# Attention in three staggered parts, with a second pair of key tiles summed on GpSimd

## The chip, the cores and the metric

The program runs on one core of one Trainium2 chip. The metric is the device time of one execution in microseconds (us). Before the change it is 2156.86 us, the median of three runs (2151.46 to 2158.35).

## The reference

One inference step of a two-layer trunk of width 1024 over 2048 latent tokens and 128 context tokens. Layer 0 mixes by latent attention (4 heads, compressed keys) and by pooling, layer 1 by a gated position mixing. What matters here is the attention of layer 0. For the latent queries it is

```
s = q_nope . k_nope + q_pe . k_pe            (keys: 2048 latent + 128 cached)
p = softmax(s * (128 + 64) ** -0.5)
o_a = p @ v                                  (per head), then o_a * silu(gate_a)
```

all in float32. Context tokens attend to context alone. In the kernel the keys and the values are the 128 wide normalised latents, and the value projection of a head (`Wuv`) comes behind the value product.

## The kernel before

The work runs in stages: projections of layer 0 (until about 523 us), attention (until about 1175 us), then output and input projections of both layers, which keep TensorE full.

Attention works on blocks of 512 queries of one head, 16 in all, and one more block for the context. A block has nine steps: steps 0 to 7 hold two tiles of 128 keys, step 8 the tile of cached keys. The context block has one step. One loop (lines 1251 to 1263) emits, for each index i, `step_scores` of step i and then `step_pv` of step i - 15 (`LAG`).

`step_scores` (line 827): five matmuls for each key tile (lines 818 to 822) into one of two PSUM pairs (psA); ScalarE copies the scores to an SBUF tile `s` (833); VectorE keeps a running maximum per key row (840, 842). After the last step VectorE joins the halves (846), GpSimd takes the maximum over the partitions (`partition_all_reduce`, 850), and ScalarE copies that to PSUM (858).

`step_pv` (line 863): VectorE subtracts the maximum (866) and ScalarE takes the exponential (870). In seven of the nine steps (`SPLIT_PV`: all but 4 and 8) the probabilities are split in two exact parts: ScalarE casts the high part (874) and GpSimd subtracts it for the low part (876, recorded as line 160 on POOL, as every subtraction of the helper `sub`). TensorE multiplies by the values in three passes (177 to 179), or in float32 (902) in steps 4 and 8, and adds up in one PSUM bank, psB. The denominator's sum over key tiles runs on VectorE in PSUM (891, 894, tile psE), except for step 1 (`POOL_SUM`), whose pair GpSimd adds (885).

`finish` (line 906), after the last step: VectorE adds the two sums (908), the sum is split (297, 160), TensorE sums over the partitions with a matrix of ones (914, 915), VectorE inverts (303 to 311), GpSimd multiplies the gate by the inverse (922), ScalarE copies the value product out of PSUM (926), TensorE applies `Wuv` (929), VectorE multiplies by the gate (939), and SP's queue stores the result (941). The gate is loaded through ScalarE's queue, the queries of the next block through GpSimd's (808, 809).

Tiles come from pools with a fixed number of buffers: 17 for `s` and the running maxima (tag h), 7 for the split probabilities and for weights (tag w), 6 for small things (tag e), 4 for queries (tag r), one PSUM bank each for B, C, D and E. Semaphores and the order on each engine come from a scheduler that plans ahead of the run with a model of each instruction's time. It prefers what stands earlier in the source, but emits what it expects to be ready; so the order on an engine can differ from that of the source, and it is fixed once the kernel is built. The first output projection is emitted in the loop's last steps, from index 145 + 9.

Of the kernel before, what the change touches and what calls it, by code (L numbers as in the profile page):

```python
# [14 lines left out]
P = 128  # L15
# [12 lines left out]
LAG = 15  # L28
# [57 lines left out]
POOL_SUM = (1,)  # L86
# [3 lines left out]
# columns of the packed per-feature vectors  # L90
# [11 lines left out]
def segments(o, n):  # L102
    """Pieces (start, length, condition) of a token block: latent tokens first, then context."""
    out = []
    if o < DEC:
        out.append((0, min(n, DEC - o), 0))
    if o + n > DEC:
        s = max(0, DEC - o)
        out.append((s, n - s, 1))
    return out  # L110
# [3 lines left out]
def trunk_kernel(ctx, tc, xT, cols_in, cond_in, ident_in, edge_in, rope_in, w_ada, w_ada_T, w_in_t, w_inp_T, w_pool,  # L114
# [54 lines left out]
    def behind(ins, last):  # L169
        """issue ins behind last, both on one engine"""  # L170
        if last is not None:
            tc.add_manual_dep(ins.ins, last.ins.name, NO_SYNC, reason="issue order")
        return ins

    def mm3(ps, w, x, first, last):
        """ps += w.T @ x with both operands split in two exact parts."""
        PE.matmul(ps, w[0], x[0], start=first, stop=False)  # L177
        PE.matmul(ps, w[0], x[1], start=False, stop=False)  # L178
        PE.matmul(ps, w[1], x[0], start=False, stop=last)  # L179

    # ---------------------------------------------------------------- constants
# [20 lines left out]
    # ---------------------------------------------------------------- scratch  # L202
# [8 lines left out]
    # ---------------------------------------------------------------- modulation  # L211
# [9 lines left out]
    def ada_derive(l, p, c):  # L221
        """what the modulation is used for: amul and gpost, of the conditions c"""
# [8 lines left out]
    def first_ada(parts):  # L231
        """shift and scale of layer 0: one piece of a weight tile at a time"""
# [30 lines left out]
    def late_ada(rows):  # L263
        """the rest of the modulation, feature by feature: rows [c] is SiLU(cond) on all partitions, in pieces"""
# [28 lines left out]
    # ---------------------------------------------------------------- statistics  # L293
    def split1(x, n, alloc, lo_eng=None):
        """[P, n] -> one tile with the high part in slot 0 and the low part in slot 1."""
# [5 lines left out]
    def invert(src, r, n, scale=None):  # L301
        """rows of src are all the same: 1/x, or 1/sqrt(x * scale + eps), once per column, into slot 1 of r."""
# [11 lines left out]
    def total(x, n, pool):  # L314
        """sum over the partitions of x [P, n], on all of them: on Pool, or prepared for TensorE."""
# [6 lines left out]
    def rstd(r, n, d, pool, tag):  # L322
        """1/sqrt(total / d + eps)"""
# [7 lines left out]
    def sumsq_tiles(tiles, n, pool):  # L331
        """sum over the 8 k-tiles (4 pair tiles) of squares."""
# [12 lines left out]
    def modulate(l, bi, tiles, r, out):  # L345
        """tiles (4 pairs, fp32, overwritten) -> split h."""
# [49 lines left out]
    def first_stats():  # L396
        """block 0: x / rms(x), before the modulation is known"""
# [24 lines left out]
    # ---------------------------------------------------------------- streamed weights  # L422
# [20 lines left out]
    def advance(k):  # L443
        """run the next k pieces of the work that trails the matrix products"""
# [10 lines left out]
    def linear_steps(hh, n, pairs, consume, hook=None):  # L455
        """pairs: number of output feature pairs; consume(pair, psum [P,2,n])"""
# [13 lines left out]
    # ---------------------------------------------------------------- layer 0, projections  # L470
    kvscope = ExitStack()
    kvp = kvscope.enter_context(tc.tile_pool(name="kvp", bufs=1))
    # keys: those of the tokens from KCUT on come late, and SiLU(cond) has their places until then
# [22 lines left out]
    def rope(raw, n, ns, tab):  # L496
        """raw [P, n]: rotate the first ns columns; result in a new tile."""
# [118 lines left out]
    def pooling(t0, t1, lo_t, hi_t, alloc=pool_tiles, size=PT):  # L616
        """o_b for tokens [t0, t1) of the sequence [lo_t, hi_t), in steps."""
# [48 lines left out]
    def merges(uq, uk, up):  # L666
# [38 lines left out]
        # cached context keys  # L705
# [80 lines left out]
    # ---------------------------------------------------------------- attention  # L786
# [17 lines left out]
    def attn_load(j):  # L804
        """queries of block j (4 blocks x 4 heads of latent tokens)."""
# [57 lines left out]
    def step_pv(b, p):  # L863
        nt = len(b.tiles[p])
        s = b.s[p]
        i = V.tensor_tensor(out=s[:, :nt], in0=s[:, :nt], in1=b.m[:, None, :].broadcast_to([P, nt, QB]),  # L866
                            op=ALU.subtract)
        if b.h is None and CTX_BEHIND:
            behind(i, g.last_fin)
        S.activation(out=s[:, :nt], in_=s[:, :nt], func=AF.Exp, scale=SM_SCALE)  # L870
        split = p in SPLIT_PV and nt == 2
        if split:
# [3 lines left out]
            sub(V if p in LO_V else G, pl[:, :nt], s[:, :nt], ph[:, :nt])  # L876
        if p == 0:
            b.o = ps1("B")
            b.pool = b.acc = None
        if nt == 1 and p == 0:  # L880
            b.acc = s[:, 0]
# [7 lines left out]
        elif b.acc is None:  # L889
            b.acc = et()[:, 0] if DEN32 else ps1("E")  # L890
            V.tensor_tensor(out=b.acc, in0=s[:, 0], in1=s[:, 1], op=ALU.add)
        else:
            for a in range(nt):
                V.tensor_tensor(out=b.acc, in0=b.acc, in1=s[:, a], op=ALU.add)  # L894
        last_p = len(b.tiles) - 1
        for a, kt in enumerate(b.tiles[p]):
            first, last = p == 0 and a == 0, p == last_p and a == nt - 1
            if split:
                i = SPLIT_PV.index(p)
                mm3(b.o, (Vh[:, i, a], Vl[:, i, a]), (ph[:, a], pl[:, a]), first, last)  # L900
            else:
                PE.matmul(b.o, Vf[:, kt] if kt < 16 else VX[:, kt - 16], s[:, a], start=first, stop=last)
        if p == last_p:
            finish(b)

    def finish(b):
        if b.pool is not None:
            g.last_fin = V.tensor_tensor(out=b.acc, in0=b.acc, in1=b.pool[:, 0], op=ALU.add)
        den = ps1("D")
        if DEN32:  # L910
            PE.matmul(den, f(ones[1]), b.acc, start=True, stop=True)
        else:
            hl = split1(b.acc, QB, et)
            PE.matmul(den, ones[1], hl[:, 0], start=True, stop=False)
            PE.matmul(den, ones[1], hl[:, 1], start=False, stop=True)
        gt = et()
        if b.h is not None:
            store(LD_GT, gt[:, 0], ga_d[b.h, :, b.t0:b.t0 + QB])
        else:
            dma(gt[:, 0].rearrange("p (h n) -> p h n", h=H), ga_d[:, :, DEC:T].rearrange("h p n -> p h n"))  # L920
        rd = invert(den[:, :QB], et(), QB)
        G.tensor_tensor(out=gt[:, 1], in0=gt[:, 0], in1=rd, op=ALU.mult)
        out = ps1("D")
        if O32:
            oh = et()
            S.copy(oh[:, 0], b.o)
            for h in ([b.h] if b.h is not None else range(H)):
                c = slice(0, QB) if b.h is not None else slice(h * P, (h + 1) * P)
                PE.matmul(out[:, c], Wuv[:, h], oh[:, 0, c], start=True, stop=True)
        elif b.h is not None:  # L930
            oh = split1(b.o, QB, et)
            mm3(out, (Wuv[:, 0, b.h], Wuv[:, 1, b.h]), (oh[:, 0], oh[:, 1]), True, True)
        else:
            oh = split1(b.o, QB, et)
            for h in range(H):
                c = slice(h * P, (h + 1) * P)
                mm3(out[:, c], (Wuv[:, 0, h], Wuv[:, 1, h]), (oh[:, 0, c], oh[:, 1, c]), True, True)
        mx = et()
        (G if MX_G else V).tensor_tensor(out=mx[:, 0], in0=out, in1=gt[:, 1], op=ALU.mult)
# [6 lines left out]
    for j in range(16):  # L946
# [3 lines left out]
        b.s = []  # L950
        b.j = j
# [4 lines left out]
    b.s = []  # L956
    b.j = 16
# [12 lines left out]
    # ---------------------------------------------------------------- layer 0 output, layer 1  # L970
# [417 lines left out]
```

## Time and profile before

| what | value |
|---|---|
| median of three runs | 2156.86 us (2151.46 to 2158.35) |
| span of the profiled execution | 2150.6 us |
| the profiled execution's own time | not stated; the timed runs lie 0.9 to 7.8 us above its span |
| TensorE matmul busy | 93% |
| VectorE busy | 74% |
| ScalarE busy | 52% |
| GpSimd busy | 27% |
| attention | 523 to 1175 us |

The span runs from the first instruction's start to the last one's end. The engines are named PE (TensorE), PEld (its weight loads), DVE (VectorE), ACT (ScalarE), POOL (GpSimd) and SP. Busy time is the sum of the instructions' durations. The ends of matmuls are modelled, and spans on POOL, of custom instructions above all, are rough. What is printed as the releaser of an idle time is inferred from semaphore events.

### The profile page before, as it was taken

How to read it: one execution, taken by the hardware profiler on the slowest of the kernel's cores; microseconds unless marked ns; L12 is line 12 of the kernel's file. 1: busy time of each engine (PE TensorE's matmuls, PEld its weight loads, DVE VectorE, ACT ScalarE, POOL GpSimd, SP SyncE). 2: the span in 40 equal slices, each digit the busy share in tenths (PEclk: the TensorE clock that was granted, in tenths of full speed). 3: DMA queues.
4: the chain of work that ended last, by engine and by line, in shares of the span. 5: the costliest groups of instructions: out<-in, count | busy, mean ns of one | idle time of the engine just before them, and what ended most of it. 6: DMA issues, size and time to landing. Idle time of an engine off the chain costs nothing. (4 is left out here: it accounts for less than half of the span.)

```text
span 2150.6 us, 25720 instructions
## 1 busy us (share of the span) xinstructions
PE 1997.9 (93%) x9442; PEld 1647.0 (77%) x9442; DVE 1589.9 (74%) x2191; ACT 1124.1 (52%) x1311; POOL 583.0 (27%) x387
## 2 busy tenths in 40 slices
PE   5998999989889899898978999999999999999997
PEld 2787777888667666676756878888878988889987
DVE  8677989765799989898987677545574657477575
ACT  6644344444566666666665444443354435445555
POOL 2102121322366575656655210011000100010010
PEclk9999999999999999999989999999999999999999
DMA  7675768766111101111114543245433533364363
GB/s 289 220 262 195 268 211 281 245 216 181 38 30 45 30 30 40 30 44 30 41 58 134 184 160 132 81 146 171 141 110 127 196 118 117 118 228 155 128 215 128
DMA packets 123119, 299.55 MB, mean 139 GB/s; under 512 B 12080, under 2 KB 39024, under 8 KB 122992
## 3 DMA queue, kind: packets, MB, share of 16 engines
q1 hardware_dynamic: 96272, 244.16, 33.6%
q0 software_dynamic: 12992, 30.15, 4.7%
q10 hardware_dynamic: 13728, 23.60, 3.5%
q8 instruction: 74, 1.21, 0.2%
q14 instruction: 53, 0.43, 0.1%
HBM read 242.18 MB, written 55.67 MB: 138 GB/s over the span
## 5 line engine op out<-in xcount | busy, mean ns | idle before, releaser
L177 PE MATMUL psA<-h,w 128*128 128x512 f32 (+2 forms) x1600 | 577.6, 361 | 14.0 <-ACT e L598 13.6
L179 PE MATMUL psA<-h,w 128*128 128x512 f32 (+2 forms) x1600 | 574.1, 359 | 4.2 <-DVE w L160 4.2
L160 DVE TENSOR_TENSOR w<-r,w 128x1024 fp32r<-128x1024 f32 x280 | 351.2, 1258 | 286.8 <-PE psA L178 193.9
L178 PE MATMUL psA<-h,w 128*128 128x512 f32 (+2 forms) x1536 | 549.0, 358 | 0.0
L431 ACT CAST w<-r 128x1024 fp32r<-128x1024 f32 x280 | 292.1, 1049 | 274.8 <-PE psA L179 192.7
L177 PEld LDWEIGHTS psA<-h,w 128*128 128x128 f32 x1600 | 303.4, 190 | 54.9 <-ACT e L598 15.4
L179 PEld LDWEIGHTS psA<-h,w 128*128 128x128 f32 x1600 | 303.4, 190 | 43.5 <-DVE w L160 5.7
L178 PEld LDWEIGHTS psA<-h,w 128*128 128x128 f32 x1536 | 291.6, 190 | 35.3 <-issue 0.5
L160 POOL TENSOR_TENSOR w<-h,w 128x1024 fp32r<-128x1024 f32 x112 | 274.6, 2467 | 116.7 <-ACT h L870 84.4
L833 ACT COPY h<-psA 128x1024 f32<-128x1024 f32 (+1 forms) x145 | 139.3, 961 | 152.0 <-PE psA L822 122.7
L870 ACT ACTIVATE h<-h 128x1024 f32<-128x1024 f32 (+1 forms) x145 | 144.7, 1008 | 57.8 <-DVE h L866 57.8
L842 DVE TENSOR_TENSOR h<-psA,h 128x1024 f32<-128x1024 f32 (+1 forms) x112 | 127.5, 1139 | 41.8 <-ACT h L833 41.7
L866 DVE TENSOR_TENSOR h<-h,psC 128x1024 f32<-128x1024 f32 x135 | 154.9, 1147 | 0.7 <-ACT psC L858 0.7
L319 POOL PARTITION_ALL_REDUCE e<-e x19 | 60.1, 3163 | 337.3 <-DVE e L977 81.2
L894 DVE TENSOR_TENSOR psE<-psE,h 128x512 f32<-128x512 f32 x208 | 143.1, 688 | 5.1 <-ACT h L870 2.0
L178 PE MATMUL psB<-w,Vh 128*128 128x512 f32 x224 | 93.2, 416 | 53.1 <-POOL w L160 53.1
L178 PE MATMUL psA<-o,w 128*128 128x512 f32 (+2 forms) x368 | 134.1, 366 | 0.0
L874 ACT CAST w<-h 128x1024 fp32r<-128x1024 f32 x112 | 117.1, 1046 | 4.8 <-PE psB L179 4.2
L179 PE MATMUL psA<-o,w 128*128 128x512 f32 (+2 forms) x304 | 109.1, 361 | 0.0
L177 PE MATMUL psA<-o,w 128*128 128x512 f32 (+2 forms) x304 | 108.9, 361 | 0.0
L177 PE MATMUL psA<-w,h 128*128 128x512 f32 x272 | 106.2, 391 | 0.5 <-ACT o L1142 0.5
L178 PE MATMUL psA<-w,h 128*128 128x512 f32 x272 | 106.1, 390 | 0.0
(290 smaller groups left out, 3641.1 us busy)
## 6 DMA issues: line engine op xcount, KB each, us to landing
r<-in_w_inc_t_dram SPq DMA_DIRECT2D x80, 512.0 KB, 3.5
r<-in_w_in_t_dram SPq DMA_DIRECT2D x60, 512.0 KB, 4.5
r<-in_w_oap_t_dram SPq DMA_DIRECT2D x40, 512.0 KB, 3.5
r<-in_w_incv_t_dram SPq DMA_DIRECT2D x40, 512.0 KB, 4.2
r<-in_w_outc_t_dram SPq DMA_DIRECT2D x40, 512.0 KB, 3.5
r<-in_w_ada_T_dram SPq DMA_DIRECT2D x32, 512.0 KB, 4.6
r<-wp_d SPq DMA_DIRECT2D x20, 512.0 KB, 6.1
h<-in_w_ada_dram SPq DMA_DIRECT2D x16, 512.0 KB, 10.2
```

The source lines that it names most:

```text
L160: eng.tensor_tensor(out=out, in0=a, in1=f(hi), op=ALU.subtract)
L177: PE.matmul(ps, w[0], x[0], start=first, stop=False)
L178: PE.matmul(ps, w[0], x[1], start=False, stop=False)
L179: PE.matmul(ps, w[1], x[0], start=False, stop=last)
L319: G.partition_all_reduce(r[:, 0, :n], x, P, bass_isa.ReduceOp.add)
L431: S.copy(hi, raw)
L833: S.copy(s[:, :nt], ps[:, :nt])
L842: V.tensor_tensor(out=b.run[:, :nt], in0=ps[:, :nt], in1=b.run[:, :nt], op=ALU.max)
L866: i = V.tensor_tensor(out=s[:, :nt], in0=s[:, :nt], in1=b.m[:, None, :].broadcast_to([P, nt, QB]), op=ALU.subtract)
L870: S.activation(out=s[:, :nt], in_=s[:, :nt], func=AF.Exp, scale=SM_SCALE)
L874: S.copy(ph[:, :nt], s[:, :nt])
L894: V.tensor_tensor(out=b.acc, in0=b.acc, in1=s[:, a], op=ALU.add)
```

## The change

`step_pv` is divided. `step_exp` does the subtraction, the exponential, the split and the denominator's sums, 13 steps behind the scores. In a block's last step it also joins the two sums, now into an SBUF tile, splits the joined sum and starts the gate's load. `step_pv` holds the value product alone, two steps behind `step_exp`. `finish` becomes a generator: the denominator, the copy of the value product and the inversion come with the last value product, and the rest (gate times inverse, `Wuv`, product, store) one index later. Step 4's pair is added on GpSimd as well, as two instructions onto the sum of step 1. Branches of settings that are not in use, and comments, are removed. The core of the diff:

```diff
-LAG = 15
+LAG = 13
+PV_BEHIND = 2
...
-POOL_SUM = (1,)
+POOL_SUM = (1, 4)
...
-    def step_pv(b, p):
+    def step_exp(b, p):
+
         nt = len(b.tiles[p])
         s = b.s[p]
-        i = V.tensor_tensor(out=s[:, :nt], in0=s[:, :nt], in1=b.m[:, None, :].broadcast_to([P, nt, QB]),
-                            op=ALU.subtract)
-        if b.h is None and CTX_BEHIND:
-            behind(i, g.last_fin)
+        V.tensor_tensor(out=s[:, :nt], in0=s[:, :nt], in1=b.m[:, None, :].broadcast_to([P, nt, QB]),
+                        op=ALU.subtract)
         S.activation(out=s[:, :nt], in_=s[:, :nt], func=AF.Exp, scale=SM_SCALE)
-        split = p in SPLIT_PV and nt == 2
-        if split:
+        b.parts[p] = None
+        if p in SPLIT_PV and nt == 2:
             ph = wt(F32R)
             S.copy(ph[:, :nt], s[:, :nt])
             pl = wt(F32R)
-            sub(V if p in LO_V else G, pl[:, :nt], s[:, :nt], ph[:, :nt])
+            sub(G, pl[:, :nt], s[:, :nt], ph[:, :nt])
+            b.parts[p] = ph, pl
         if p == 0:
-            b.o = ps1("B")
             b.pool = b.acc = None
+        last_p = len(b.tiles) - 1
         if nt == 1 and p == 0:
-            b.acc = s[:, 0]
+            b.total = s[:, 0]
         elif p in POOL_SUM:
             if b.pool is None:
                 b.pool = et()
...
                 for a in range(2):
                     G.tensor_tensor(out=b.pool[:, 0], in0=b.pool[:, 0], in1=s[:, a], op=ALU.add)
         elif b.acc is None:
-            b.acc = et()[:, 0] if DEN32 else ps1("E")
+            b.acc = ps1("E")
             V.tensor_tensor(out=b.acc, in0=s[:, 0], in1=s[:, 1], op=ALU.add)
         else:
             for a in range(nt):
                 V.tensor_tensor(out=b.acc, in0=b.acc, in1=s[:, a], op=ALU.add)
+        if p == last_p:
+            if b.acc is not None:
+                t = et()
+                V.tensor_tensor(out=t[:, 0], in0=b.acc, in1=b.pool[:, 0], op=ALU.add)
+                b.total = t[:, 0]
+            b.hl = split1(b.total, QB, et)
+            b.gt = et()
+            if b.h is not None:
+                store(LD_GT, b.gt[:, 0], ga_d[b.h, :, b.t0:b.t0 + QB])
+            else:
+                dma(b.gt[:, 0].rearrange("p (h n) -> p h n", h=H), ga_d[:, :, DEC:T].rearrange("h p n -> p h n"))
+
+    def step_pv(b, p):
+        if p == 0:
+            b.o = ps1("B")
         last_p = len(b.tiles) - 1
         for a, kt in enumerate(b.tiles[p]):
-            first, last = p == 0 and a == 0, p == last_p and a == nt - 1
-            if split:
+            first, last = p == 0 and a == 0, p == last_p and a == len(b.tiles[p]) - 1
+            if b.parts[p]:
                 i = SPLIT_PV.index(p)
+                ph, pl = b.parts[p]
                 mm3(b.o, (Vh[:, i, a], Vl[:, i, a]), (ph[:, a], pl[:, a]), first, last)
             else:
-                PE.matmul(b.o, Vf[:, kt] if kt < 16 else VX[:, kt - 16], s[:, a], start=first, stop=last)
-        if p == last_p:
-            finish(b)
+                PE.matmul(b.o, Vf[:, kt] if kt < 16 else VX[:, kt - 16], b.s[p][:, a], start=first, stop=last)
+        b.parts[p] = None
 
     def finish(b):
-        if b.pool is not None:
-            g.last_fin = V.tensor_tensor(out=b.acc, in0=b.acc, in1=b.pool[:, 0], op=ALU.add)
+
         den = ps1("D")
-        if DEN32:
-            PE.matmul(den, f(ones[1]), b.acc, start=True, stop=True)
-        else:
-            hl = split1(b.acc, QB, et)
-            PE.matmul(den, ones[1], hl[:, 0], start=True, stop=False)
-            PE.matmul(den, ones[1], hl[:, 1], start=False, stop=True)
-        gt = et()
-        if b.h is not None:
-            store(LD_GT, gt[:, 0], ga_d[b.h, :, b.t0:b.t0 + QB])
-        else:
-            dma(gt[:, 0].rearrange("p (h n) -> p h n", h=H), ga_d[:, :, DEC:T].rearrange("h p n -> p h n"))
+        PE.matmul(den, ones[1], b.hl[:, 0], start=True, stop=False)
+        PE.matmul(den, ones[1], b.hl[:, 1], start=False, stop=True)
+        oh = et()
+        S.copy(oh[:, 0], b.o)
         rd = invert(den[:, :QB], et(), QB)
+        gt = b.gt
+        yield
         G.tensor_tensor(out=gt[:, 1], in0=gt[:, 0], in1=rd, op=ALU.mult)
         out = ps1("D")
-        if O32:
-            oh = et()
-            S.copy(oh[:, 0], b.o)
-            for h in ([b.h] if b.h is not None else range(H)):
-                c = slice(0, QB) if b.h is not None else slice(h * P, (h + 1) * P)
-                PE.matmul(out[:, c], Wuv[:, h], oh[:, 0, c], start=True, stop=True)
-        elif b.h is not None:
-            oh = split1(b.o, QB, et)
-            mm3(out, (Wuv[:, 0, b.h], Wuv[:, 1, b.h]), (oh[:, 0], oh[:, 1]), True, True)
-        else:
-            oh = split1(b.o, QB, et)
-            for h in range(H):
-                c = slice(h * P, (h + 1) * P)
-                mm3(out[:, c], (Wuv[:, 0, h], Wuv[:, 1, h]), (oh[:, 0, c], oh[:, 1, c]), True, True)
+        for h in ([b.h] if b.h is not None else range(H)):
+            c = slice(0, QB) if b.h is not None else slice(h * P, (h + 1) * P)
+            PE.matmul(out[:, c], Wuv[:, h], oh[:, 0, c], start=True, stop=True)
         mx = et()
-        (G if MX_G else V).tensor_tensor(out=mx[:, 0], in0=out, in1=gt[:, 1], op=ALU.mult)
+        V.tensor_tensor(out=mx[:, 0], in0=out, in1=gt[:, 1], op=ALU.mult)
         if b.h is not None:
             store(ST_MX, mix_d[b.h, :, b.t0:b.t0 + QB], mx[:, 0])
         else:
...
-    for i in range(len(steps) + LAG):
+    finishing = []
+    for i in range(len(steps) + LAG + PV_BEHIND + 1):
         if i < len(steps):
             b, p = steps[i]
             nb = blks.index(b) + 1
...
             step_scores(b, p)
         if i >= POOL_AT:
             drain(pools, 1)
-        if i >= LAG:
-            step_pv(*steps[i - LAG])
+        if 0 <= i - LAG < len(steps):
+            step_exp(*steps[i - LAG])
+        for it in list(finishing):
+            if next(it, it) is it:
+                finishing.remove(it)
+        j = i - LAG - PV_BEHIND
+        if 0 <= j < len(steps):
+            b, p = steps[j]
+            step_pv(b, p)
+            if p == len(b.tiles) - 1:
+                finishing.append(finish(b))
+                next(finishing[-1])
         if i >= len(steps) + OA_AT:
             drain(first, 1)
```

## Rows read from the trace of the kernel before

**Rows 1.** The page of the kernel before: span, and busy time of each engine

```profile
span 2150.6 us, 25720 instructions
...
PE 1997.9 (93%) x9442; PEld 1647.0 (77%) x9442; DVE 1589.9 (74%) x2191; ACT 1124.1 (52%) x1311; POOL 583.0 (27%) x387
```

**Rows 2.** Stretches of attention: PE, PEld, DVE, ACT, POOL busy (x), PEclk, DMA share, GB/s

```profile
523.00:1175.00 652.00, 575.44 (x2270) 425.37 (x2269) 574.65 (x639) 417.43 (x464) 387.25 (x237) 0.97 0.15 45
1100.00:1175.00 75.00, 58.42 (x214) 40.39 (x213) 62.54 (x72) 43.07 (x50) 45.38 (x22) 0.86 0.35 114
```

**Rows 3.** Table by stretches: one steady block, from reduction to reduction

```profile
703.30:740.82 37.52, 34.12 (x139) 25.49 (x138) 34.29 (x39) 25.20 (x29) 22.91 (x12) 1.00 0.12 35
```

**Rows 4.** Waits of 523 to 1175 us: us in total, times, longest

```profile
POOL w L160 <- ACT h L870: 84.4, 12, 7.2
POOL e L850 <- DVE psE L894: 77.7, 13, 6.2
...
PE psB L178 <- POOL w L160: 53.1, 31, 7.6
```

**Rows 5.** Timeline of GpSimd, 695 to 742 us: start, us, what [idle before <-releaser]

```profile
695.01 2.38 POOL L160 TENSOR_TENSOR w<-h,w 128x1024 fp32r<-128x1024 f32 x1 [0.43 <-ACT w L874]
703.30 1.80 POOL L850 PARTITION_ALL_REDUCE e<-e  x1 [5.91 <-DVE psE L894]
712.25 9.88 POOL L160 TENSOR_TENSOR w<-h,w 128x1024 fp32r<-128x1024 f32 x4 [7.15 <-ACT h L870]
722.44 2.40 POOL L160 TENSOR_TENSOR w<-h,w 128x1024 fp32r<-128x1024 f32 x1 [0.31 <-POOL w L160]
725.25 1.30 POOL L922 TENSOR_TENSOR e<-e,e 128x512 f32<-128x512 f32 x1 [0.41 <-DVE e L311]
726.75 2.41 POOL L160 TENSOR_TENSOR w<-h,w 128x1024 fp32r<-128x1024 f32 x1 [0.20 <-PE psB L178]
729.11 1.31 POOL L885 TENSOR_TENSOR e<-h 128x512 f32<-128x512 f32 x1
730.53 0.90 POOL L808 DMA_DIRECT2D r<-q_d  x1
731.44 0.58 POOL L809 DMA_DIRECT2D r<-q_d  x1
732.46 2.38 POOL L160 TENSOR_TENSOR w<-h,w 128x1024 fp32r<-128x1024 f32 x1 [0.44 <-ACT w L874]
740.82 1.81 POOL L850 PARTITION_ALL_REDUCE e<-e  x1 [5.98 <-DVE psE L894]
749.38 9.88 POOL L160 TENSOR_TENSOR w<-h,w 128x1024 fp32r<-128x1024 f32 x4 [6.75 <-ACT h L870]
```

**Rows 6.** The line of the all-reduce: duration ns min/median/max, first and last start

```profile
L850 POOLq MODIFY_POOL_CONFIG  x32: 1/1/54, 547.2 to 1112.5; - x32
L850 POOL PARTITION_ALL_REDUCE e<-e x16: 1803/1803/1807, 553.7 to 1118.4; - x16
```

**Rows 7.** Groups by shape, 500 to 1150 us: busy us, mean ns | idle before

```profile
L894 DVE TENSOR_TENSOR psE<-psE,h 128x512 f32<-128x512 f32 x206 | 141.7, 688 | 5.1 <-ACT h L870 2.0
...
L885 POOL TENSOR_TENSOR e<-h 128x512 f32<-128x512 f32 x16 | 20.8, 1301 | 0.0
...
L160 DVE TENSOR_TENSOR e<-psE,e 128x512 fp32r<-128x512 f32 x15 | 10.2, 679 | 1.3 <-ACT e L297 1.3
```

**Rows 8.** The line of the last maximum: duration ns min/median/max

```profile
L846 DVE TENSOR_TENSOR e<-h x16: 675/2793/4380, 547.4 to 1110.3; 128x512 f32<-128x512 f32 x16
```

**Rows 9.** Timeline of VectorE: from a block's last maximum to its first use

```profile
695.15 2.79 DVE L846 TENSOR_TENSOR e<-h 128x512 f32<-128x512 f32 x1
...
706.45 1.21 DVE L866 TENSOR_TENSOR h<-h,psC 128x1024 f32<-128x1024 f32 x1
```

**Rows 10.** Timeline of GpSimd at the end of attention

```profile
1128.71 2.35 POOL L160 TENSOR_TENSOR w<-h,w 128x1024 fp32r<-128x1024 f32 x1 [6.70 <-ACT w L874]
...
1152.29 3.37 POOL L160 TENSOR_TENSOR h<-e,h 128x1024 fp32r<-128x1024 f32 x1
```

More of the change, by code (lines that the diff above doesn't have):

```diff
@@ L950, in trunk_kernel @@
         b.s = []
+        b.parts = {}
         b.j = j
@@ L956, in trunk_kernel @@
     b.s = []
+    b.parts = {}
     b.j = 16
```

## The prediction

> **What bounds the kernel now.** I read the page first, to see where the stage of the change lies: the span is 2150.6 us and TensorE is busy for 93% of it, so over the whole program TensorE looks like the limit [rows 1]. Then the table by stretches, for attention alone (523 to 1175 us): there TensorE, with its modelled ends, shows 575 of 652 us, VectorE as much, ScalarE 417 and GpSimd 387 [rows 2]. One steady block of queries (nine steps) takes 37.52 us, with 34.12 on TensorE, 34.29 on VectorE and 22.91 on GpSimd [rows 3]. By these shares GpSimd has nearly 15 us free in each block. The waits contradict that: the longest TensorE waits in the stage are for GpSimd's low parts (53.1 us over 31 waits), while GpSimd itself seems to wait 84.4 and 77.7 us, about as often as there are blocks [rows 4]. An engine that others wait for and that itself waits needs a look at its own timeline [rows 5].
>
> That timeline is the heart of the matter. The low part at 695.01 ends at 697.39; the all-reduce of the maxima is shown at 703.30 for 1.80 us; the next low part starts at 712.25. The 5.91 us before it and the 7.15 us after it are printed as waits, the first for a VectorE sum, which the reduction does not need. The same two gaps stand at the next block: 5.98 and 6.75 us [rows 5]. Two pool-configuration instructions belong to each reduction (32 for 16) [rows 6]; the gaps are equal from block to block within 0.4 us, whatever is going on around them. I take them as GpSimd switching its code to the reduction and back, and so as occupied: 712.25 - 697.39 = 14.86 us per block. The rest of the cycle, from 712.25 to 734.84, is seven low parts, two sums or products of 1.30 us and two DMA issues, with idle bits of 0.31, 0.41, 0.20, 0.11 and 0.44 us, together 1.47 us [rows 5]. So GpSimd works for 36.0 of 37.5 us: **GpSimd sets the pace of attention**, at 96%, and TensorE and VectorE follow.
>
> The label of the trace would have it otherwise, so I weigh it against a rule: the Trainium skill, GPSIMD Engine Reference, section Instruction dispatch, says that the first call to freshly loaded code pays a load of about 6 us (5.95) after the pool-configuration instruction, with no visible instruction. By it the gaps are work and the added sums lengthen each block, as in my sum; by the label they are waits and the sums fit into them, which is the first rival below. The trace's 5.91 and 5.98 us agree with the figure.
>
> **The change, part by part.**
> *One more pair on GpSimd.* For each of 16 blocks, VectorE loses two sums into psE (L894, 0.69 us each) and GpSimd gains two of the kind of L885 and L922, 1.30 us each [rows 5, 7]: +2.6 us of GpSimd per block, 41.6 us in all. Nothing covers it except the 1.47 us of idle bits. The VectorE gain, 16 x 2 x 0.69 = 22 us, lies on an engine that has 3.2 us idle per block already and buys nothing while GpSimd leads.
>
> *The total and its split.* The last addition now writes an SBUF tile and the split reads that tile, where it read psE. The subtraction in the split (L160 on VectorE, e<-psE,e, 0.68 us [rows 7]) so gets two SBUF inputs. The trace has such an instruction: L846 took between 0.68 and 4.38 us, 2.79 in the middle [rows 8]; one that started at 695.15 [rows 9], with a GpSimd low part running until 697.39 [rows 5], ended at 697.94. So VectorE can pay from 0 to 2.1 us per block, inside its 3.2 us. GpSimd pays too when it comes second: its low parts took 2.35 us alone and 3.37 us at the end of the stage, where VectorE made such subtractions [rows 10]. I take +0.4 us per block on GpSimd (the four of 712.25 took 9.88 where 4 x 2.35 is 9.40 [rows 5, 10], a block with other such instructions), bounds 0 and 1.0.
> The Trainium skill, SBUF — State Buffer, section Who interferes with whom, says that a VectorE instruction with two SBUF inputs and a GpSimd instruction that reads SBUF exclude each other for a whole instruction; by it the split costs one engine or the other up to a GpSimd instruction, by the row of the old form it costs nothing. The trace's 2.79 beside 0.68 us agree with the rule.
>
> *Value product two steps later.* The same matmuls. The casts and low parts stay with the exponentials; TensorE gets two steps (2 x 37.5 / 9 = 8.3 us) in the source between a low part and its use. That can remove waits of TensorE for GpSimd, up to the 53 us of [rows 4], but they are the shadow of GpSimd's pace: with less delay TensorE would wait elsewhere. Gain 0. The low and high parts live longer in the seven w buffers; three pairs and one tile fit, and three pairs is what the new distance needs, so the buffers fill. If a low part must wait for a product of three steps before, GpSimd idles: bounds 0 and the present 0.31 us twice per block; I take 0.
>
> *Lag 15 to 13.* Maxima would be ready five steps ahead of use rather than seven. The engines do not follow the source order here: seven steps would be 29 us, but L846 stands at 695.15 and the first subtraction of that maximum at 706.45, 11.3 us later, right behind the reduction [rows 9]. So I cost the lag at nothing in the steady part; the prologue and the drain lose two steps each and the middle gains two, about -2 us.
>
> *Block ending in pieces.* The product with the gate (L922) stands a step later, so its 0.41 us wait for VectorE's transpose [rows 5] goes: -0.4 us per block. The gate load moves two steps forward in ScalarE's queue, where casts and exponentials stand behind it; if its e buffer were not free, they would wait. ScalarE is idle for a third of the stage [rows 2], the old issue showed no wait, and I take 0, with one step (4.2 us) per block as the far upper bound, not in the range. The copy of the value sum (ScalarE, before: after the inversion) frees its PSUM bank sooner; TensorE has room, gain 0. The store of the result stays on SP's queue, one step later, with nobody near behind it.
>
> *Sum.* Per block 2.6 + 0.4 - 0.4 = 2.6 us, in 16 blocks 41.6. At the end, TensorE has about 75 - 58.4 = 16.6 us idle between 1100 and 1175 [rows 2], where products of the following projection can move ahead while GpSimd finishes; I count 5 us for that and 2 for the lag. **41.6 - 7 = +35 us.** The profiled span is 2150.6 us; the timed runs lie 0.9 to 7.8 us above it, the median 6.3. The page states no other time of the profiled execution, so I add the difference to the median: 2156.9 + 35 = **2192 us**. Nothing after attention changes.
>
> **The rivals.**
> *GpSimd's gaps are real waits* (faster). Then there are 14.6 us free per block, the sums hide, and VectorE bounds: 34.3 - 1.4 + about 1.2 for the split, 34.1, plus half its present idle, gives a 35.5 us block, -2.0 x 15 = -30: 2127 us. For it: the printed labels. Against: two gaps of constant length, at each reduction. Chance 0.11.
> *The idle bits and the end absorb it* (no change). If all 1.47 us per block vanish (23.5 us) and all of TensorE's 16.6 us idle at the end is filled, 41.6 - 40 = +1.5: 2158 us. For it: most bits are waits on casts or buffers, which a looser order can remove. Against: they recur as short handovers of 0.1 to 0.4 us. It decides only if both come together. Chance 0.09.
> *The total waits behind a reduction* (slower still). The new sums of step 4 may be queued on GpSimd behind the next block's reduction, 14.9 us; the total, on VectorE four steps later, about 16.6 us, then stands still with the next subtractions behind it, and GpSimd runs dry after its backlog of low parts, about two (4.8 us). It decides once the sums stand behind the reduction by more than those 1.7 us. Price: some 2.5 us per block more, 15 x 2.5 = 37: 2229 us. For it: L885 of step 1 already runs late, at 729.11, after five low parts [rows 5]. Chance 0.15.
> *The new distances change no order on the engines.* Then the added sums and the split remain, and the time is the forecast's; it has no number of its own.
>
> **How the numbers follow.** Forecast 0.65, rivals 0.11, 0.09 and 0.15. The forecast's own range is 2172 (the idle bits gone, -20) to 2210 (a split at 1.0 us, +10, and a slower clock at the end, which already is 0.86 in [rows 2], +8). The range takes in the no-change case almost to its number and the third rival: 2160 to 2233. A measurement tells about 0.3% (6.5 us) from no change; faster by more 0.11, within 0.09, slower by more 0.80.
>
> **What would show it.** On GpSimd's timeline, two more sums per block between reductions and a distance of about 40 us from reduction to reduction; the gaps around each reduction again near 6 and 7 us; VectorE's and TensorE's idle per block longer by about 2 us; L160 on VectorE with e<-e above 0.68 us. I am wrong if the period falls below 37.5 us with the two sums in it, or if the gaps around a reduction shrink.

## The result and the profile after

The changed kernel takes 2191.66 us (median of 4 runs, 2191.25 to 2193.67), the kernel before beside it 2155.62 us. The ratio is 1.0167, with a 95% interval of 1.0150 to 1.0184: slower by 36 us. The profiled execution has a span of 2189.6 us, 39.0 us more than before. A span lies about 2 us under the time of its execution (2189.6 under 2191.39), so by estimate the profiled execution of the kernel before took 2152.5 us, 3 us less than its median; that is the difference between 39.0 and 36.

The page of the changed kernel, its span and the busy time of each engine:

```profile
span 2189.6 us, 25719 instructions
...
PE 2015.3 (92%) x9442; PEld 1662.4 (76%) x9442; DVE 1553.7 (71%) x2159; ACT 1127.8 (52%) x1311; POOL 612.4 (28%) x419
```

VectorE has 32 instructions less and GpSimd 32 more, which is the pair of step 4 in 16 blocks. VectorE is 36 us less busy, GpSimd 29 us more, and the program is longer [rows 1]. The table by stretches, one steady block and the last 75 us of attention (columns as in [rows 2]):

```profile
874.66:913.53 38.87, 33.77 (x138) 25.48 (x138) 31.96 (x37) 25.32 (x29) 24.82 (x14) 1.00 0.12 35
1140.00:1215.00 75.00, 56.72 (x190) 38.05 (x191) 51.21 (x58) 38.00 (x44) 35.57 (x18) 0.86 0.35 113
```

The block is 38.87 us where it was 37.52 [rows 3]. VectorE's busy time fell from 34.29 to 31.96 us in it; what it gained became idle time. GpSimd's timeline in the same block of the changed kernel:

```profile
874.66 1.80 POOL L851 PARTITION_ALL_REDUCE e<-e  x1 [5.99 <-DVE e L899]
883.20 4.75 POOL L161 TENSOR_TENSOR w<-h,w 128x1024 fp32r<-128x1024 f32 x2 [6.74 <-ACT h L834]
887.89 1.30 POOL L886 TENSOR_TENSOR e<-h 128x512 f32<-128x512 f32 x1
889.15 4.76 POOL L161 TENSOR_TENSOR w<-h,w 128x1024 fp32r<-128x1024 f32 x2
893.87 2.65 POOL L889 TENSOR_TENSOR e<-e,h 128x512 f32<-128x512 f32 x2
896.47 2.41 POOL L161 TENSOR_TENSOR w<-h,w 128x1024 fp32r<-128x1024 f32 x1
898.83 1.30 POOL L932 TENSOR_TENSOR e<-e,e 128x512 f32<-128x512 f32 x1
900.08 2.39 POOL L161 TENSOR_TENSOR w<-h,w 128x1024 fp32r<-128x1024 f32 x1
902.40 0.90 POOL L809 DMA_DIRECT2D r<-q_d  x1
903.31 0.59 POOL L810 DMA_DIRECT2D r<-q_d  x1
905.17 2.40 POOL L161 TENSOR_TENSOR w<-h,w 128x1024 fp32r<-128x1024 f32 x1 [1.27 <-ACT w L874]
913.53 1.80 POOL L851 PARTITION_ALL_REDUCE e<-e  x1 [5.96 <-DVE e L899]
```

It answers to [rows 5]. The two new sums (L889) take 2.65 us. The gaps on both sides of the reduction are what they were, 5.99 and 6.74 us, with other instructions now printed as their cause. Between them GpSimd stands still for 1.27 us only; the 0.41 us in front of the product with the gate (L932, before L922) are gone. The reductions of all blocks, from the line of the all-reduce in the changed kernel (duration min/median/max, first and last start):

```profile
L851 POOL PARTITION_ALL_REDUCE e<-e x16: 1801/1802/1804, 554.5 to 1150.1; - x16
```

From the start of the first to the start of the last of 16 reductions there are (1150.1 - 554.5) / 15 = 39.71 us a block; before it was (1118.4 - 553.7) / 15 = 37.65 us [rows 6]. That makes 15 x 2.06 = 30.9 us. The first reduction starts 0.8 us later. From the last reduction's start to the end of the span there were 2150.6 - 1118.4 = 1032.2 us; now there are 1039.5, so 7.3 us more. 30.9 + 0.8 + 7.3 = 39.0 us. I call the two parts the **period** (the mean length of a block) and the **end** below, and take them from each run's own lines in the same way.

Three waits of the changed kernel (all of attention; us in total, times, longest):

```profile
DVE e L938 <- POOL e L932: 62.4, 15, 6.8
PE psB L179 <- POOL w L161: 42.9, 21, 5.9
DVE h L868 <- ACT psC L859: 13.2, 13, 4.0
```

TensorE's wait for low parts fell from 53.1 [rows 4] to 42.9 us, without any gain in time. The first one is new in size (6.9 us before): VectorE reaches the product with the gate earlier than GpSimd does.

### The profile page after: what moved, and what is told of

It is laid out like the page before. It is cut to its first block, busy times and chain, and to the rows that moved or that the text cites. A ratio compares the mean times of both kernels' runs of the same rounds, so it can differ in the third digit from the quotient of the medians.

```text
span 2189.6 us, 25719 instructions
## 1 busy us (share of the span) xinstructions
PE 2015.3 (92%) x9442; PEld 1662.4 (76%) x9442; DVE 1553.7 (71%) x2159; ACT 1127.8 (52%) x1311; POOL 612.4 (28%) x419
## 5 line engine op out<-in xcount | busy, mean ns | idle before, releaser
L161 POOL TENSOR_TENSOR w<-h,w 128x1024 fp32r<-128x1024 f32 x112 | 266.5, 2389 | 124.2 <-ACT h L870 34.8
L868 DVE TENSOR_TENSOR h<-h,psC 128x1024 f32<-128x1024 f32 x135 | 153.2, 1150 | 13.2 <-ACT psC L859 13.2
L179 PE MATMUL psB<-w,Vh 128*128 128x512 f32 x224 | 98.3, 439 | 42.9 <-POOL w L161 42.9
L895 DVE TENSOR_TENSOR psE<-psE,h 128x512 f32<-128x512 f32 x176 | 121.6, 691 | 9.5 <-ACT h L870 7.1
L874 ACT CAST w<-h 128x1024 fp32r<-128x1024 f32 x112 | 117.3, 1047 | 18.1 <-PE psB L180 17.1
L819 PE MATMUL psA<-r,K 128*128 128x512 f32 x192 | 87.8, 457 | 40.0 <-DVE h L843 39.7
L178 PE MATMUL psA<-w,h 128*128 128x512 f32 x272 | 106.2, 391 | 0.4 <-ACT o L1143 0.4
```

The costliest lines, as they stand in the source:

```text
L161: eng.tensor_tensor(out=out, in0=a, in1=f(hi), op=ALU.subtract)
L819: PE.matmul(ps, kh, q[0], start=True, stop=False)
L874: S.copy(ph[:, :nt], s[:, :nt])
```

## The experiments

Each is compared with the kernel before, run beside it on the same chip. Ratios carry 95% intervals.

**1. The pair back on VectorE.**

```diff
-POOL_SUM = (1, 4)
+POOL_SUM = (1,)
```

> The changed kernel with step 4's pair back on VectorE, so lag, stagger, split of the total and the ending in pieces remain. Theory (GpSimd sets the pace and the two added sums are the cost): the block loses 2.6 us of GpSimd, 40 us in all, and the time returns to about the kernel before, 2150 to 2160 us. Rival (the stagger, the lag or the SBUF total cost the time): it stays near 2190 us.

2168.17 us, 1.0069 (1.0049 to 1.0088). The pair is worth about 21 of the 36 us, so it is the larger cost, but the rest of the change costs about 15 us by itself: neither expectation held alone. The line of its reductions shows where:

```profile
L851 POOL PARTITION_ALL_REDUCE e<-e x16: 1802/1802/1803, 555.5 to 1121.2; - x16
```

The period is 37.71 us, as before. With a span of 2167.3 us its end is 1046.1 us, 13.9 longer than before. The lag, the stagger, the total and the pieces together do nothing to the steady part and lengthen what follows the last reduction.

**2. The pair on GpSimd in the kernel before.**

```diff
-POOL_SUM = (1,)
+POOL_SUM = (1, 4)
```

> The kernel before with nothing changed but step 4's pair on GpSimd. Theory: +2.6 us per block less what its 1.47 us of idle bits absorb, 20 to 42 us, so 2176 to 2198 us. Rival (the new distances are the cost, and GpSimd has room): within 6 us of 2156.

2206.63 us, 1.0245 (1.0228 to 1.0261): more than the theory allowed, and slower than the changed kernel. The reductions, and the waits of attention that grew:

```profile
L850 POOL PARTITION_ALL_REDUCE e<-e x16: 1802/1802/1803, 553.2 to 1165.8; - x16
```

```profile
ACT psC L858 <- POOL e L850: 108.0, 15, 9.6
DVE h L866 <- ACT psC L858: 94.8, 13, 9.1
```

The period is 40.84 us, 3.2 more than before, where two sums are 2.6. VectorE now waits 94.8 us for the maxima (0.7 before, 13.2 in the changed kernel). In GpSimd's queue the sums stand in front of the next block's reduction:

```profile
716.70 1.80 POOL L850 PARTITION_ALL_REDUCE e<-e  x1 [6.29 <-PE psA L822]
725.53 9.47 POOL L160 TENSOR_TENSOR w<-h,w 128x1024 fp32r<-128x1024 f32 x4 [7.04 <-ACT h L870]
736.71 1.29 POOL L922 TENSOR_TENSOR e<-e,e 128x512 f32<-128x512 f32 x1 [1.71 <-DVE e L311]
...
741.89 2.67 POOL L888 TENSOR_TENSOR e<-e,h 128x512 f32<-128x512 f32 x2
...
757.87 1.80 POOL L850 PARTITION_ALL_REDUCE e<-e  x1 [6.65 <-PE psA L822]
```

This block is 41.17 us long, 3.65 more than that of [rows 5]. The two sums are 2.67 of it, the gaps around the reduction about 0.6 (7.04 and 6.65 us for 7.15 and 5.98), and GpSimd's idle bits 0.2: 1.71 us in one wait for VectorE's inversion, for 1.47 in five bits. So the sums were added in full and no idle bit took them in. VectorE's wait for the maxima lies on an engine that is busy for 30.37 of the 41.17 us; no run shows that it costs time by itself.

**3. A second, unused reduction in each block.**

```diff
+    g.extra = qpool.tile([P, P], F32, name="extra")
...
-            sub(V if p in LO_V else G, pl[:, :nt], s[:, :nt], ph[:, :nt])
+            lo = G.tensor_tensor(out=pl[:, :nt], in0=s[:, :nt], in1=f(ph[:, :nt]), op=ALU.subtract)
+            if p == 2:
+                behind(G.partition_all_reduce(g.extra, ident, P, bass_isa.ReduceOp.max), lo)
```

> The kernel before with a second, unused all-reduce of a constant 128x128 tile in each of 16 blocks, queued on GpSimd behind the low part of step 2; nothing waits for it but GpSimd's own queue. Theory (the gaps on both sides of a reduction are GpSimd changing its code): 13 to 15 us more per block, +190 to +230 us. Rival (the gaps are waits for data): only the instruction itself, at most 1.8 us per block, so at most +29 us.

2344.88 us, 1.0891 (1.0870 to 1.0911): +191 us, where waits would have given 29 at most. Around one of the added reductions:

```profile
816.17 0.72 POOL L879 PARTITION_ALL_REDUCE extra<-ident  x1 [5.92 <-issue]
823.66 1.28 POOL L888 TENSOR_TENSOR e<-h 128x512 f32<-128x512 f32 x1 [6.77 <-issue]
```

The instruction takes 0.72 us and reads a constant, and still it has 5.92 us before it and 6.77 us behind it: 13.4 us, in which nothing was there to wait for. The gaps are GpSimd's own time. This settles the reading of [rows 5] on which the forecast stands. The 5.92 us agree with the load of about 6 us that the Trainium skill, GPSIMD Engine Reference, section Instruction dispatch, gives for the first call to freshly loaded code. Here such a time falls on each change of code, in both directions.

**4. No reduction.**

```diff
-            ar = G.partition_all_reduce(m[:, 1], src, P, bass_isa.ReduceOp.max)
...
-                b.m = m[:, 1]
+                b.m = src
...
-                S.copy(b.m, m[:, 1])
+                S.copy(b.m, src)
```

> The kernel before without the all-reduce: each partition's own maximum is used, so the maximum over the partitions is left out. Theory: GpSimd has 14.9 us less per block and no longer leads; the next engine, VectorE at about 34 us a block, sets the pace: -2 to -4 us per block, 2095 to 2125 us. Rival (gaps are waits, something else sets the pace): less than 10 us faster.

2115.54 us, 0.9821 (0.9806 to 0.9836), as the theory expected. A stretch of 34.5 us in its steady part shows what leads then, VectorE at 33.96 and TensorE at 33.35 us (columns as in [rows 2]):

```profile
700.00:734.50 34.50, 33.35 (x137) 25.35 (x137) 33.96 (x36) 25.58 (x29) 22.97 (x12) 1.00 0.14 39
```

**5. The block ending in one piece.**

```diff
     def finish(b):
+        yield from ()
...
         gt = b.gt
-        yield
...
-                next(finishing[-1])
+                next(finishing[-1], None)
```

> The changed kernel with the block ending in one piece again, two sums on GpSimd kept. The trace after the change shows VectorE held 62.4 us by the product with the gate on GpSimd (L932), 15 times. If GpSimd's pace is what counts, this wait is a shadow and the time stays within 6 us of 2192; if the pieces cause the drain's extra 10 us, it comes to about 2180 us.

2195.5 us, 1.0184 (1.0150 to 1.0217), not told from the changed kernel's 1.0167. The ending in pieces neither costs nor gains, and the pieces are not what the end lost. VectorE's wait for the gate's product is still there, 59.0 us over 15 times, so this run doesn't show what it would give to be rid of it; that it is a shadow of GpSimd's pace is argued, not shown.

**6. No stagger, the pair moved.**

```diff
-LAG = 13
-PV_BEHIND = 2
+LAG = 15
+PV_BEHIND = 0
```

> The changed kernel with LAG 15 and PV_BEHIND 0: no distance between exponential and value product; the total in SBUF, the pieces and the two sums on GpSimd stay. Theory (in the steady part GpSimd sets the pace, and the old order lets the reduction wait behind the two sums, as in the kernel before with the pair moved, 2206.6 us): about 2200 us, so the stagger is worth 10 us or more where the pair is moved. Rival (the stagger costs the drain 15 us and nothing else): about 2177 us.

2213.37 us, 1.0258 (1.0233 to 1.0284), more than the expected 2200. The stagger and the shorter lag save about 20 us where the pair is moved, nearly all of it in the period (40.91 for 39.71 us). Two waits of this run:

```profile
POOL w L161 <- PE psB L179: 33.9, 13, 5.3
DVE h L868 <- ACT psC L859: 64.0, 13, 7.4
```

The first is on the engine that leads: low parts wait for a value product of TensorE, once in nearly every block. In the changed kernel this is 0.7 us, and waits of low parts for their cast (L874) take its place with 18.0 us. The difference, 15 us, is most of the 18 us that the period gives. The second, VectorE's wait for the maxima (13.2 us in the changed kernel), comes with it; whether it stands behind the first isn't shown.

**7. Lag 13 in the kernel before.**

```diff
-LAG = 15
+LAG = 13
```

> The kernel before with LAG 13 alone. Theory (the engines' order follows readiness, and GpSimd sets the pace): within 8 us of 2154. Rival (the lag is what costs the changed kernel without the moved pair its 15 us): about 2168 us.

2169.86 us, 1.0063 (1.0040 to 1.0086): the rival. The reductions run from 553.6 to 1120.9 us, a period of 37.82 us, and the span is 2163.9, so the end is 1043.0 us, 10.8 more than before; by the medians the run is 12.5 us longer. Here, too, the steady part is what it was. In this kernel the loop is two indices shorter and gives the output projection four pieces instead of six; the changed kernel gives it seven and its end is still longer than before, so that alone is not the cause.

**8. Five split steps in the kernel before.** Steps 3 and 7 go through TensorE in float32.

```diff
-SPLIT_PV = (0, 1, 2, 3, 5, 6, 7)
+SPLIT_PV = (0, 1, 2, 5, 6)
```

> The kernel before with steps 3 and 7 in float32 instead of three passes of split operands: two low parts fewer per block on GpSimd (4.9 us), two casts fewer on ScalarE (2.1 us), 0.7 us more on TensorE. Theory (GpSimd leads at 36 us of 37.5): it falls to 31 us, VectorE leads at about 34.2 us a block, and the time falls by 2.5 to 3.3 us per block, to 2100 to 2115 us, faster than both kernels. Rival (TensorE leads): 0.7 us more per block, about 2165 us.

2119.11 us, 0.9826 (0.9798 to 0.9853): faster than both kernels, 4 us short of the expected gain. One steady block:

```profile
876.75:910.90 34.15, 33.84 (x134) 24.92 (x133) 31.39 (x39) 23.38 (x26) 17.69 (x10) 1.00 0.14 39
```

It takes 34.15 us, and TensorE, with its modelled ends, fills 33.84 of them, VectorE 31.39: with GpSimd relieved, TensorE leads, not VectorE as expected. Over all blocks the period is (1086.5 - 549.6) / 15 = 35.79 us, since the first blocks and the last two are longer.

**9. Lag 15 without stagger, the pair back.** Experiments 1 and 6 together, so that only the total in SBUF and the pieces remain of the change.

> The changed kernel with the pair back on VectorE and with LAG 15 and PV_BEHIND 0, so that only the total in SBUF and the ending in pieces remain of the change. If the lag and the stagger cost the drain its 10 us and more (the changed kernel with the pair back took 2168 us), this returns to about 2156 us. If the pieces or the total do, it stays at about 2168 us.

2160.26 us over 10 runs, 1.0014 (0.9998 to 1.0030). This is not told from the kernel before; against the 1.0069 of experiment 1, lag and stagger make up most of the 15 us. The total and the pieces alone cost nothing that these runs can tell.

**10 to 12. Five split steps with the other settings.** The line of experiment 8 in the changed kernel, in the kernel before with the pair moved, and in the changed kernel with the pair back.

> The changed kernel with steps 3 and 7 in float32, both pairs on GpSimd. GpSimd has about 38.6 - 4.9 = 33.7 us a block, VectorE about 33, TensorE 33.5, so the theory gives about 35.5 us a block with all three near their limit: -4.2 us from the changed kernel's 39.7, about 2125 to 2135 us. If the moved pair pays once GpSimd no longer leads, it is at or below the 2119 us of the kernel before with the same five splits.

> The kernel before with steps 3 and 7 in float32 and step 4's pair on GpSimd. Theory: with 2.6 us more GpSimd has 33.7 us a block and VectorE 1.4 us less, so the moved pair now costs little or nothing against 2119 us: 2110 to 2125 us. If the sums are dear by their place in the queue and not by GpSimd's load, it costs 20 us or more: about 2140 us.

> The changed kernel with steps 3 and 7 in float32 and step 4's pair back on VectorE. GpSimd then has 31 us a block. If the pair on GpSimd costs here too, this is 10 to 25 us below the 2133 us with it: 2108 to 2123 us. If VectorE, relieved by the moved pair, is what counts once GpSimd has room, it is slower than 2133 us.

Measured: 2133.04 us, 0.9884 (0.9860 to 0.9907); 2145.01 us, 0.9943 (0.9917 to 0.9968); 2132.35 us, 0.9882 (0.9866 to 0.9899). The last two missed their expectation: experiment 11 came near its rival (about 2140 us), experiment 12 was no faster than 10. Without the stagger the moved pair costs 26 us even where GpSimd has room (35.79 to 36.99 us a block); with the stagger it costs nothing (35.70 and 35.65 us). GpSimd's queue shows why. One block of experiment 8, and one of experiment 11, from reduction to reduction:

```profile
876.75 1.80 POOL L850 PARTITION_ALL_REDUCE e<-e  x1 [6.13 <-ACT e L297]
...
895.64 1.30 POOL L922 TENSOR_TENSOR e<-e,e 128x512 f32<-128x512 f32 x1 [3.07 <-DVE e L311]
...
910.90 1.80 POOL L850 PARTITION_ALL_REDUCE e<-e  x1 [6.10 <-ACT e L297]
```

```profile
851.45 1.80 POOL L850 PARTITION_ALL_REDUCE e<-e  x1 [6.05 <-PE psA L822]
...
870.41 1.30 POOL L922 TENSOR_TENSOR e<-e,e 128x512 f32<-128x512 f32 x1 [2.95 <-DVE e L311]
...
875.41 2.68 POOL L888 TENSOR_TENSOR e<-e,h 128x512 f32<-128x512 f32 x2
...
888.31 1.80 POOL L850 PARTITION_ALL_REDUCE e<-e  x1 [6.44 <-DVE h L840]
```

GpSimd stands about 3 us for VectorE's inversion in both. From the reduction to the gate's product it is 18.89 and 18.96 us; from there to the next reduction 15.26 and 17.90. The new sums stand behind that wait and in front of the reduction, so the block grows by all of their length though GpSimd is idle for 3 us of it. VectorE's side closes the ring: it starts on the new maximum and works through to the inversion.

```profile
853.91 2.35 DVE L866 TENSOR_TENSOR h<-h,psC 128x1024 f32<-128x1024 f32 x2 [2.21 <-ACT psC L858]
...
869.63 0.70 DVE L311 STREAM_TRANSPOSE e<-s 128x512 f32<-128x512 f32 x1
```

With the stagger the sums stand in front of the gate's product and fill the wait. In experiment 12 GpSimd waits 2.17 us there; in experiment 10 the sums end as the product starts:

```profile
897.77 1.30 POOL L932 TENSOR_TENSOR e<-e,e 128x512 f32<-128x512 f32 x1 [2.17 <-DVE e L312]
```

```profile
893.67 2.63 POOL L889 TENSOR_TENSOR e<-e,h 128x512 f32<-128x512 f32 x2
896.25 1.29 POOL L932 TENSOR_TENSOR e<-e,e 128x512 f32<-128x512 f32 x1
```

Periods and ends, each from the profiled execution's own line of reductions and its span. That execution's time stands beside the median:

| kernel | split steps | pair of step 4 | median us | profiled us | period us | end us |
|---|---|---|---|---|---|---|
| before | 7 | VectorE | 2156 | not stated | 37.65 | 1032.2 |
| changed | 7 | GpSimd | 2192 | 2191.4 | 39.71 | 1039.5 |
| 1: changed, pair back | 7 | VectorE | 2168 | 2169.1 | 37.71 | 1046.1 |
| 2: before, pair moved | 7 | GpSimd | 2207 | 2205.7 | 40.84 | 1038.1 |
| 5: changed, in one piece | 7 | GpSimd | 2196 | 2204.3 | 39.99 | 1044.0 |
| 6: changed, no stagger | 7 | GpSimd | 2213 | 2208.7 | 40.91 | 1040.9 |
| 7: before, lag 13 | 7 | VectorE | 2170 | 2165.7 | 37.82 | 1043.0 |
| 9: changed, no stagger, pair back | 7 | VectorE | 2160 | 2166.4 | 37.79 | 1041.0 |
| 8: before | 5 | VectorE | 2119 | 2118.7 | 35.79 | 1030.4 |
| 10: changed | 5 | GpSimd | 2133 | 2133.8 | 35.65 | 1042.5 |
| 11: before, pair moved | 5 | GpSimd | 2145 | 2147.5 | 36.99 | 1035.7 |
| 12: changed, pair back | 5 | VectorE | 2132 | 2134.0 | 35.70 | 1043.9 |

An end is that of one execution, and executions of one kernel differ by up to 14 us here (2152.36 to 2166.44 in experiment 9). The profile of the kernel before is of an execution some 3 us under its median; those of experiments 5 and 9 are the slowest of their runs, 9 and 6 us above it. So the ends of 5 and 9 don't show that they are longer than before, and a difference of a few us between two ends shows nothing.

## Why the prediction was right, and which of its terms were not

The forecast of 2192 us was met by 2191.66. The engine that leads, the gaps and the two sums were right; that the number was met to the microsecond is luck, by two errors of opposite sign: the steady part was 41.6 in the sum and about 31 us in the trace, the end was -7 and is +7.3 in the profiles (about +4 by the medians).

**GpSimd sets the pace: right.** Experiments 3, 4 and 8 show it from three sides: more work on GpSimd lengthens the program nearly one for one (13.4 us in 16 blocks would be 214, measured 191), and less of it shortens the program until another engine leads. In the late blocks of the changed kernel GpSimd stands still for 1.27 of 38.9 us. The gaps printed as waits are work.

**The two sums, +2.6 us a block: right in size** (2.65 us in the timeline). The step counted them as load alone. Their place in the queue counts too once GpSimd has room: behind its wait for the inversion they cost all of their length (experiment 11), in front of it nothing (experiment 10).

**The split of the total, +0.4 us a block on GpSimd: wrong in sign.** GpSimd's low parts became shorter, as the groups by shape of the changed kernel's attention show (busy us, mean ns | idle before):

```profile
L161 POOL TENSOR_TENSOR w<-h,w 128x1024 fp32r<-128x1024 f32 x112 | 266.5, 2389 | 124.2 <-ACT h L870 34.8 <-ACT h L834 34.1 <-PE psA L823 21.0
L161 DVE TENSOR_TENSOR e<-e,e 128x512 fp32r<-128x512 f32 x16 | 14.2, 889 | 0.0
L892 DVE TENSOR_TENSOR psE<-h 128x512 f32<-128x512 f32 x16 | 11.1, 692 | 0.0
```

The 112 low parts took 274.6 us on the page before and take 266.5 now, 0.5 us a block less. The split with two SBUF inputs takes 0.889 us on VectorE (0.679 before [rows 7]), and the first sum of the denominator, which has two SBUF inputs as well and took 1.62 us on average in the kernel before (L891), is down to 0.692. Experiment 7 has the shorter low parts by the lag alone (268.5 us), so it is not the split's doing. In the changed order the two mostly stand where no low part runs beside them. VectorE's timeline of the block above has them between the start of the reduction (874.66) and the next low part (883.20):

```profile
875.49 0.76 DVE L161 TENSOR_TENSOR e<-e,e 128x512 fp32r<-128x512 f32 x1
...
880.52 0.69 DVE L892 TENSOR_TENSOR psE<-h 128x512 f32<-128x512 f32 x1
```

By the Trainium skill, SBUF — State Buffer, section Who interferes with whom, a VectorE instruction with two SBUF inputs and a GpSimd instruction that reads SBUF exclude each other. The trace agrees: the last maximum (L847, two SBUF inputs) starts at 905.50 in the same block, beside a low part that ends at 907.57, and takes 2.62 us. I had not asked when the two engines would meet.

**The gate's product, -0.4 us a block: right.** So a block should take 2.65 - 0.5 - 0.4 = 1.7 us more, and the late blocks do, near 38.9 us for 37.4. Earlier blocks are longer, which brings the mean to 39.71. The longest of the steady ones:

```profile
634.73:675.83 41.10, 33.23 (x116) 24.64 (x115) 30.21 (x35) 24.98 (x28) 24.76 (x14) 0.88 0.11 32
```

In the four blocks from 634.73 to 795.74 GpSimd stands still for 1.9 to 2.9 us, for 1.27 in the late ones. In three of them TensorE's mean granted clock is 0.88 to 0.92, so part of them ran at 1.2 GHz instead of 2.4; they are 40.1 to 41.1 us long, the fourth, at 1.00, 39.5. The kernel before has 1.00 in all its steady blocks, with TensorE busy for 34.12 of 37.52 us [rows 3]. Whether the slower clock lengthened these blocks or came of their idle time isn't shown.

**The value product two steps later, gain 0: wrong where the pair is moved.** Experiment 6 prices the stagger with its lag at about 20 us; on GpSimd it is the wait of low parts for value products that goes, 33.9 to 0.7 us, for 18.0 us of waits on casts. With the pair on VectorE the steady part gains nothing, as forecast.

**Lag 13, -2 us, and the end, -5 us: wrong.** The lag alone costs 12.5 us by the medians; the profiles have 10.8 us of it behind the last reduction. In the changed kernel TensorE idles no less in the last 75 us (56.72 us busy, for 58.42 in [rows 2]), so nothing was filled. The loss is made in the first 150 us behind the last reduction, here before and after the change:

```profile
1118.40:1268.40 150.00, 133.89 (x548) 103.45 (x549) 110.86 (x128) 78.47 (x89) 51.67 (x24) 0.93 0.44 144
1150.10:1300.10 150.00, 128.73 (x517) 97.45 (x518) 101.50 (x120) 77.44 (x86) 46.69 (x25) 0.94 0.42 135
```

TensorE runs 31 matmuls fewer there, and 695 in the next 150 us of either; at that rate 31 are 6.7 of the 7.3 us. Experiments 1 and 7 run 495 and 500. What in the new order holds TensorE back there is open. In front of the last two products with the gate GpSimd waits 8.02 and 8.28 us for VectorE's inversion before, and 14.10 and 11.44 us in experiment 1, but no run shows that TensorE's loss hangs on that. I didn't try other places for the start of the output projection.

**The rivals.** The first (real waits) fell with experiment 3. Its sum had a slip: 34.1 us plus half of 3.2 is 35.7 us a block, not 35.5, so its time is 2130 us. The second (absorption) did not come: the idle bits stayed at 1.3 us in the late blocks. The third named a reduction in front of the sums; in the block above the sums stand in front of the reduction (887.89 and 893.87, reduction at 913.53), and VectorE's wait for the maxima stayed at 13.2 us in all. Of the signs, the period, the gaps and the split (0.889 us) came as said, and TensorE's idle time (5.1 for 3.4 us a block); VectorE's grew by 3.7 us, not 2.

## What to carry to other kernels

Before an engine is called free, look at its own timeline around instructions that need other code: idle time that is the same in every round, whatever else goes on, is work. Move work off the engine that leads (here two split steps, for 38 us), not onto it, and ask of each added instruction what stands behind it in its queue, and whether it can stand in front of a wait instead. Changes of order in a steady loop also move its end, so price the drain by itself.

## What the runs showed of the hardware that was not expected

A change of code on GpSimd costs in both directions, about 5.9 us before the first instruction of the new kind and 6.8 us before the next ordinary one, for an instruction of 0.72 as of 1.80 us. Two reductions that stand next to each other share it: at the end of attention in the changed kernel the second starts as the first one ends.

```profile
1150.12 1.80 POOL L851 PARTITION_ALL_REDUCE e<-e  x1 [5.79 <-DVE psE L895]
1151.84 1.87 POOL L851 PARTITION_ALL_REDUCE e<-h  x1
```

A float32 product of a pair of key tiles in place of three passes on split operands cost TensorE so little that two splits fewer in a block gave the fastest of the kernels that compute the whole result: TensorE's busy time in a steady block, with modelled ends, was 33.84 us, for 34.12 before [rows 3].
